# Two weight tiles of w_up split ahead of w_out's last rows, and one pair of attention heads scored a weight tile later, in a one-core hybrid decoder layer

## The chip, the cores and the metric

The kernel runs on one core of one Trainium2 chip. The metric is the time of one execution on the device in microseconds (us); the median of several runs is compared. TensorE is called PE here (PEld is its weight load), VectorE DVE, ScalarE ACT, GpSimd POOL; SP only issues transfers.

## What is computed

One decoder layer on 256 tokens of width 2048, all in float32. A norm, one wide projection, a state-space group and an attention group side by side, a second projection, a residual with a norm, and a squared-ReLU MLP:

```python
mix = hybrid_mixer(rmsnorm(h, norm_mix_pre), w_in, ..., w_out)   # concat(SSD, attention) @ w_out
h = h + rmsnorm(mix, norm_mix_post)
ff = squared_relu_mlp(rmsnorm(h, norm_mlp_pre), w_up, w_down)    # relu(u @ w_up)^2 @ w_down
h = h + rmsnorm(ff, norm_mlp_post)
...
s = where(mask, q @ k^T, -inf)          # attention: scores,
p = exp(s - max(s)); o = p @ v / sum(p) # probabilities, products with the values
```

w_in is 2048 x 12320, w_out 4096 x 2048, w_up 2048 x 8192, w_down 8192 x 2048.

## The kernel before

Every large product is made in split form. A float32 weight tile of 256 rows x 512 columns (two blocks of 128 rows) is fetched into a raw buffer, ACT rounds it to fp32r (hi, L144) and DVE takes the rest (lo, L145); the activations are kept as hi and lo too. A product is then hi*hi + hi*lo + lo*hi. There are four raw buffers (RAWS) and five pairs of hi and lo (BUFS). A raw buffer is free when DVE has made lo; a hi buffer is free when PE has done the matmuls that read it. SP issues the fetches in the order of the tiles.

Products come in two shapes. With features on the partitions (gemm_features, L474), one weight tile is sixteen matmuls, eight with hi (L468) and eight with lo (L471). With tokens on the partitions (row_tile, L317), one weight tile and one half of the tokens are six matmuls (L323 to L325).

**Where the attention is worked in.** gemm_features ends each of its eight weight tiles with pump(n): n pieces of waiting work are issued, and each piece that has more to do goes to the end of the queue. A pair of heads (attention, L842) is three pieces: scores (PE, L849 and L850, into two small PSUM buffers), followed by mask and maximum (DVE, L857), exponentials and their sums (ACT, L859), reciprocal and scaling (DVE, L861 and L863); then the transposes of the probabilities (PE, L871) and their copies (ACT, L875); then the products with the values (PE, L880 and L881) and their split. heads puts two such pairs into the queue. The small PSUM buffers are two, and they go round: the transposes of the first pair take those that the scores of the second pair filled. The tuple of pumps at L991, q2, says after which weight tiles of the queries' product a piece is issued; it repeats when it is shorter than eight. Other places have tuples of their own and are as they were.

**Where w_out passes over to w_up.** mix_to_up (L1055) ends w_out's last block of 512 columns and begins w_up. Its order is written out by hand and kept by every engine. It is made of small helpers: out(t, i) is the i-th of the last four weight tiles of w_out for half t of the tokens (tiles 2 and 3 lie in the buffer ua, which later holds the new activations); mix(t, n) adds the finished columns (DVE, L1080); mix_square takes their sum of squares (ACT, L1084); scale_of makes the mean (DVE, L1023) and its power -1/2 (POOL, L1024); weight multiplies by the norm's weights (L1087); add makes the new h (DVE, L1091); turn transposes it (PE, L1100); take splits it into the activations (ACT L146, DVE L147); rows(t, i) is a tile of w_up's first block. weigh(i) fetches w_up's tile i and splits it (ACT L144, DVE L145).

Of the kernel before, what the change touches and what calls it, by code (L numbers as in the profile page):

```python
# [35 lines left out]
COL_Q = COL_DT + 32  # L36
COL_K = COL_Q + NH * DH
COL_V = COL_K + NH * DH
NB = 512
# [38 lines left out]
def hymba_layer(ctx: ExitStack, tc: tile.TileContext, x, norm_mix_pre, w_in, conv_w, conv_b, dt_bias, a_log,  # L78
# [24 lines left out]
    def u(k):  # L103

        t, i = us[k]
        return t[:, i]
# [206 lines left out]
    def drain():  # L313
        while waiting:
            pump()
# [158 lines left out]
    def gemm_features(src, c0, begun=None, pumps=(1,)):  # L474


        acc = features()
        for k0 in range(0, NK, KB):
            hi, lo = weights(src, k0, c0) if k0 or begun is None else begun

            edges = k0 in (0, NK - KB)
            for fs in [(f,) for f in range(4)] if edges else [range(4)]:
                products(acc, hi, lo, k0, [(f, j) for f in fs for j in range(KB)])
            pump(pumps[k0 // KB % len(pumps)])
        return acc

    def added(dst, acc):

        with tc.high_priority(offset=AHEAD):
            for f, a in enumerate(acc):  # L490
                nc.scalar.activation(dst[:, f], a[:, 1], AF.Copy)
                nc.vector.tensor_tensor(dst[:, f], a[:, 0], dst[:, f], op=ALU.add)
# [139 lines left out]
    rbq = fp.tile([P, S], F32, name="rbq")  # L632
# [251 lines left out]
    def queries(c0, scale, pumps=(1,)):  # L884
        acc = gemm_features(w_in, c0, pumps=pumps)
        dst = mp.tile([P, 4, S], F32, name="cT", bufs=5)
        for b in range(2):
            d = dst[:, 2 * b:2 * b + 2]
            added(d, acc[2 * b:2 * b + 2])
            nc.vector.tensor_tensor(d, d, scale[:, None, :].to_broadcast([P, 2, S]), op=ALU.mult)  # L890
        return dst
# [76 lines left out]
    def heads(hb, qT, kT, v):  # L968
        for j in (0, 2):
            waiting.append(attention(ap, 4 * hb + j, qT[:, j:j + 2], kT[:, j:j + 2],  # L970
                                     v[:, :, j * DH:(j + 2) * DH].rearrange("p t (j d) -> p t j d", j=2)))
# [16 lines left out]
    qk.append(keys_by_tokens(1, (0, 2, 1, 4, 3, 7, 5), (6,), *eight))  # L988
    vs = two_values(0, *eight[::-1])
    heads(0, *qk[0], vs[0])  # L990
    q2 = queries(COL_Q + 2 * NB, rbq, (1, 1, 0))  # L991
    drain()
    heads(1, *qk[1], vs[1])
    qk.append((q2, queries(COL_K + 2 * NB, rbc, (1, 1, 0))))
# [19 lines left out]
    def sums_but_last(sums, t):  # L1014

        some = cp.tile([P, 1], F32, name="some", bufs=4)
        nc.vector.tensor_reduce(some, sums[:, t, 0:3], axis=mybir.AxisListType.X, op=ALU.add)
        nc.vector.tensor_scalar(some, some, D * EPS, None, op0=ALU.add)
        return some
# [35 lines left out]
    def mix_to_up(c0, ks, acc):  # L1055


        up = [bank() for _ in range(NT)]
        banks, turned = [], {}
        weighed = hp.tile([P, NT, NB], F32, name="e")  # L1060
        room_w = big.tile([P, SUMS, 2, S], F32R, name="ua").rearrange("p k b s -> p k (b s)")

        def tile_of(src, k, c0, at=None):
            raw = fetch(src, k * KB, c0)
            hi, lo = parts() if at is None else (room_w[:, at + KB * i:at + KB * (i + 1)] for i in range(2))
            split(hi, lo, raw)
            return hi, lo

        def out(t, i):
            row_tile(acc[1 + 2 * t], t, o[i], ks[i], part, False, i == len(ks) - 1)  # L1070

        def weigh(i):
            w[i] = tile_of(w_up, i % 8, i // 8 * NB)

        def rows(t, i):
            row_tile(up[t], t, w[i], i, act_u, i == 0, i == NK // KB - 1)

        def mix(t, n):
            m = mw_at(t, columns(n))
            nc.vector.tensor_tensor(m, acc[n - 2 + 2 * t], m, op=ALU.subtract if n % 2 else ALU.add)  # L1080

        def mix_square(t, n):
            junk = hp.tile([P, NB], F32, name="junk")
            nc.scalar.activation(junk, mw_at(t, columns(n)), AF.Square, accum_out=ssq[:, t, n:n + 1])  # L1084

        def weight(t, n):
            nc.vector.tensor_mul(mw_at(t, columns(n)) if n == 2 else weighed[:, t], mw_at(t, columns(n)), wpost[n])  # L1087

        def add(t, n):
            cs = columns(n)  # L1090
            nc.vector.scalar_tensor_tensor(of_h(t, cs), weighed[:, t] if n == 3 else mw_at(t, cs), rm[:, t:t + 1],  # L1091
                                           of_h(t, cs), op0=ALU.mult, op1=ALU.add)

        def turn(t, n):
            if len(banks) < 3:
                banks.append([bank() if banks else psmall() for _ in range(2)])
            p = turned[t, n] = banks[len(turned) % 3]
            for f in range(4):
                k = 4 * n + f
                nc.tensor.transpose(p[f % 2][:, f // 2 * P:(f // 2 + 1) * P], of_h(t, slice(k * P, (k + 1) * P)), ident)  # L1100

        def take(t, i):
            for k in (2 * i, 2 * i + 1):
                f = k % 4
                split(*(u(k)[:, b, t * P:(t + 1) * P] for b in range(2)),
                      turned[t, k // 4][f % 2][:, f // 2 * P:(f // 2 + 1) * P], w_mlp[:, k:k + 1])

        def square(t, n):
            junk = hp.tile([P, NB], F32, name="junk")
            nc.scalar.activation(junk, of_h(t, columns(n)), AF.Square, accum_out=ssh[:, t, n:n + 1])  # L1110

        o, w = {}, {}
        with tc.high_priority(offset=AHEAD), tc.manual_schedule():
            o[0] = tile_of(w_out, ks[0], c0)
            with tc.issue_after(product[0].ins), tc.issue_after(product[1].ins):
                out(0, 0)
            o[1] = tile_of(w_out, ks[1], c0)
            out(0, 1)
            o[2] = tile_of(w_out, ks[2], c0, 0)
            o[3] = tile_of(w_out, ks[3], c0, 4)  # L1120
            mix(0, 2)
            mix_square(0, 2)
            out(0, 2)
            mix(1, 2)
            mix_square(1, 2)
            first3[0] = sums_but_last(ssq, 0)
            first3[1] = sums_but_last(ssq, 1)
            out(0, 3)
            mix(0, 3)
            weight(0, 2)  # L1130
            weigh(0)
            out(1, 0)
            mix_square(0, 3)
            out(1, 1)
            scale_of(rm, ssq, first3[0], 0)
            weigh(1)
            add(0, 0)
            out(1, 2)
            add(0, 1)
            turn(0, 0)  # L1140
            weigh(2)
            square(0, 0)
            out(1, 3)
            new_u()
            take(0, 0)
            square(0, 1)
            mix(1, 3)
            turn(0, 1)
            take(0, 1)
            take(0, 2)  # L1150
            rows(0, 0)
            mix_square(1, 3)
            rows(0, 1)
            scale_of(rm, ssq, first3[1], 1)
            add(0, 2)
            take(0, 3)
            add(1, 0)
            weigh(3)
            square(0, 2)
            weight(1, 3)  # L1160
            rows(0, 2)
            add(1, 1)
            square(1, 0)
            turn(1, 0)
            turn(0, 2)
            take(1, 0)
            rows(0, 3)
            take(0, 4)
            take(1, 1)
            turn(1, 1)  # L1170
            rows(1, 0)
            square(1, 1)
            rows(1, 1)
            weight(1, 2)
            take(1, 2)
            add(1, 2)
            weigh(4)
            turn(1, 2)
            add(1, 3)
            take(0, 5)  # L1180
            take(1, 3)
            rows(1, 2)
            rows(0, 4)
            turn(1, 3)
            square(1, 2)
            weight(0, 3)
            add(0, 3)
            take(1, 4)
            rows(1, 3)
            weigh(5)  # L1190
            take(1, 5)
            weigh(6)
            turn(0, 3)
            rows(1, 4)
            rows(0, 5)
            take(1, 6)
            square(0, 3)
            weigh(7)
            take(0, 6)
            rows(1, 5)  # L1200
            take(0, 7)
            square(1, 3)
            rows(1, 6)
            scale_of(rmlp, ssh, sums_but_last(ssh, 0), 0)
            rows(0, 6)
            weigh(8)
            take(1, 7)
            rows(0, 7)
            rows(1, 7)
            scale_of(rmlp, ssh, sums_but_last(ssh, 1), 1)  # L1210
        for t in range(NT):
            waiting.append(first_hidden(t, up[t]))
        pump(NT)
        return w[8]
# [247 lines left out]
```

## Time and profile before

| | us |
|---|---|
| median of 3 runs | 1464.41 (1463.12 to 1464.65) |
| the profiled execution | 1462.01 |
| its span, first to last instruction | 1460.1 |
| PE busy | 1451.3 (99%) |
| DVE busy | 1254.7 (86%) |
| ACT busy | 888.7 (61%) |
| POOL busy | 143.1 (10%) |

The granted clock of PE is 0.999 of full speed over the whole span. A timeline row gives start, duration, engine, line, operation, what it writes and reads, and in brackets the idle time ahead of it with what ended it. Times count from the span's start. The attention of the first two pairs lies at about 447 to 473 us, the passage from w_out to w_up at about 757 to 800 us.

### The profile page before, as it was taken

The numbers are of one execution on the slowest core, as the hardware profiler recorded it, in microseconds if no ns is written. First come the engines' busy times: TensorE is split into PE (matmuls) and PEld (weight loads), VectorE is DVE, ScalarE is ACT, GpSimd is POOL, SyncE is SP. The second block draws the span as 40 slices with busy tenths as digits, with TensorE's granted clock in tenths as the row PEclk, the third lists the DMA queues.
The fourth block names the chain that finished last, engine by engine and source line by source line (L and its number), as shares of the span: only waits on it lengthen the run. The fifth ranks groups of instructions, "written<-read, shape, count | busy, mean of one in ns | idle before, by whom it ended". The sixth has DMA issues, their size and how long they took to land.

```text
span 1460.1 us, 20264 instructions
## 1 busy us (share of the span) xinstructions
PE 1451.3 (99%) x7129; PEld 1223.8 (84%) x7129; DVE 1254.7 (86%) x1864; ACT 888.7 (61%) x1214; POOL 143.1 (10%) x208
## 2 busy tenths in 40 slices
PE   9999999999999999999999999999999999999998
PEld 8888888888888888888887888888888888888886
DVE  6798797898887686689979999988889999999987
ACT  7475675465566555555557677655455776766553
POOL 0003100212010000000100011000111111001000
PEclk9999999999999999999999999999999999999999
DMA  8766666666886586688867798778888888797763
GB/s 273 209 204 180 180 184 192 175 180 184 226 241 206 134 245 199 192 265 253 253 190 241 202 315 240 217 214 230 246 236 271 263 244 250 204 308 238 251 212 116
DMA packets 168039, 323.53 MB, mean 222 GB/s; under 512 B 15185, under 2 KB 18113, under 8 KB 167937
## 3 DMA queue, kind: packets, MB, share of 16 engines
q1 hardware_dynamic: 144448, 272.37, 59.0%
q0 software_dynamic: 15616, 36.19, 12.3%
q10 hardware_dynamic: 7872, 13.68, 2.8%
q8 instruction: 56, 0.92, 0.2%
q14 instruction: 47, 0.38, 0.1%
HBM read 317.96 MB, written 40.41 MB: 245 GB/s over the span
## 4 chain that ended last, share of the span: by engine, by line
PE 99%; DVE 1%; ACT 0%; issue 0%; POOL 0%
PE acc L468 15%; PE acc L323 12%; PE acc L325 12%; PE acc L324 12%; PE acc L471 8%; PE acc L408 6%; PE acc L407 6%; PE acc L406 6%; PE ps L325 3%; PE ps L323 3%; PE ps L324 3%; PE ps L406 2%; PE ps L408 2%; PE ps L407 2%; PE ps L802 1%; PE acc L1375 1%
## 5 line engine op out<-in xcount | busy, mean ns | idle before, releaser
L144 ACT ACTIVATE hi<-raw 128x1024 fp32r<-128x1024 f32 (+1 forms) x408 | 427.1, 1051 | 293.0 <-PE acc L325 93.9
L145 DVE TENSOR_TENSOR lo<-raw,hi 128x1024 fp32r<-128x1024 f32 (+1 forms) x408 | 496.2, 1220 | 103.8 <-ACT hi L144 99.2
L468 PE MATMUL acc<-ua,hi 128*128 128x512 f32 x600 | 163.4, 401 | 0.0
L468 PEld LDWEIGHTS acc<-ua,hi 128*128 128x128 f32 x600 | 105.7, 189 | 16.7
L144 ACT ACTIVATE hi<-e 128x1024 fp32r<-128x1024 f32 x61 | 64.9, 1063 | 73.8 <-DVE e L247 67.4
L323 PE MATMUL acc<-hi,ua 128*128 128x512 f32 x248 | 98.5, 397 | 0.0
L471 PEld LDWEIGHTS acc<-ua,lo 128*128 128x128 f32 x600 | 88.2, 189 | 10.2
L325 PE MATMUL acc<-hi,ua 128*128 128x512 f32 x248 | 96.8, 390 | 0.0
L324 PE MATMUL acc<-lo,ua 128*128 128x512 f32 x248 | 96.7, 390 | 0.0
L471 PE MATMUL acc<-ua,lo 128*128 128x256 f32 x600 | 90.8, 281 | 0.0
L323 PE MATMUL acc<-hi,sh 128*128 128x512 f32 x224 | 88.4, 395 | 0.0
L325 PE MATMUL acc<-hi,sl 128*128 128x512 f32 x224 | 87.3, 390 | 0.0
L324 PE MATMUL acc<-lo,sh 128*128 128x512 f32 x224 | 87.2, 389 | 0.0
L145 DVE TENSOR_TENSOR lo<-e,hi 128x1024 fp32r<-128x1024 f32 x61 | 74.2, 1217 | 0.0
L468 PE MATMUL acc<-uc,hi 128*128 128x512 f32 x240 | 68.4, 397 | 0.0
L406 PE MATMUL acc<-hi,ah 128*128 128x512 f32 x166 | 64.7, 389 | 0.0
L407 PE MATMUL acc<-lo,ah 128*128 128x512 f32 x166 | 64.6, 389 | 0.0
L408 PE MATMUL acc<-hi,al 128*128 128x512 f32 x166 | 64.6, 389 | 0.0
L325 PE MATMUL acc<-hi,al 128*128 128x512 f32 x148 | 57.6, 389 | 0.0
L323 PE MATMUL acc<-hi,ah 128*128 128x512 f32 x148 | 57.6, 389 | 0.0
L324 PE MATMUL acc<-lo,ah 128*128 128x512 f32 x148 | 57.6, 389 | 0.0
L325 PEld LDWEIGHTS acc<-hi,ua 128*128 128x128 f32 x248 | 46.6, 188 | 10.0
(533 smaller groups left out, 3436.4 us busy)
## 6 DMA issues: line engine op xcount, KB each, us to landing
raw<-in_w_in_dram SPq DMA_DIRECT2D x181, 512.0 KB, 4.0
raw<-in_w_down_dram SPq DMA_DIRECT2D x73, 512.0 KB, 5.0
raw<-in_w_up_dram SPq DMA_DIRECT2D x65, 512.0 KB, 4.8
raw<-in_w_out_dram SPq DMA_DIRECT2D x39, 512.0 KB, 4.9
pair<-in_w_up_dram POOLq DMA_DIRECT2D x56, 256.0 KB, 5.3
raw<-pair SPq DMA_DIRECT2D x46, 256.0 KB, 4.5
pair<-in_w_down_dram POOLq DMA_DIRECT2D x46, 256.0 KB, 5.9
ha<-in_w_up_dram SPq DMA_DIRECT2D x20, 512.0 KB, 5.1
```

Of the source, the lines that this page charges most:

```text
L144: return (nc.scalar.activation(hi, src, AF.Copy), nc.vector.tensor_tensor(lo, src, hi.bitcast(F32), op=ALU.subtract))
L145: nc.vector.tensor_tensor(lo, src, hi.bitcast(F32), op=ALU.subtract))
L323: nc.tensor.matmul(dst, a_h[:, r, ts], hi[:, j], start=begin and j == 0, stop=False)
L324: nc.tensor.matmul(dst, a_h[:, r, ts], lo[:, j], start=False, stop=False)
L325: product[t] = nc.tensor.matmul(dst, a_l[:, r, ts], hi[:, j], start=False, stop=end and j == KB - 1)
L406: nc.tensor.matmul(dst, a_h, hi[:, j], start=own and first, stop=False)
L407: nc.tensor.matmul(dst, a_h, lo[:, j], start=False, stop=False)
L408: nc.tensor.matmul(dst, a_l, hi[:, j], start=False, stop=own and last)
L468: nc.tensor.matmul(acc[f], hi[:, j, f * P:(f + 1) * P], u(k0 + j), start=k0 + j == 0, stop=False, skip_group_check=True)
L471: nc.tensor.matmul(acc[f][:, 0], lo[:, j, f * P:(f + 1) * P], u(k0 + j)[:, 0], start=False, stop=k0 + j == NK - 1, skip_group_check=True)
L802: nc.tensor.matmul(p[:, c, r], bc[:, r, c * P:(c + 1) * P], xdt[:, c, r], start=True, stop=True)
L1375: nc.tensor.transpose(p[:, f * P:(f + 1) * P], r[:, f * P:(f + 1) * P], ident)
```

## The change

Two edits. In heads(0), which shares the queries' product q2, the pieces are issued after other weight tiles. Numbered from 0, before the first pair's pieces came after tiles 0, 3 and 6 and the second pair's after 1, 4 and 7; now the second pair's come after 2, 5 and 7, and the first pair's stay. In mix_to_up, weigh(0) and weigh(1) are issued ahead of out(0, 3), not behind weight(0, 2) and scale_of.

```diff
     heads(0, *qk[0], vs[0])
-    q2 = queries(COL_Q + 2 * NB, rbq, (1, 1, 0))
+    q2 = queries(COL_Q + 2 * NB, rbq, (1,0,1,1,0,1,1,1))
     drain()
...
             first3[0] = sums_but_last(ssq, 0)
             first3[1] = sums_but_last(ssq, 1)
+            weigh(0)
+            weigh(1)
             out(0, 3)
             mix(0, 3)
             weight(0, 2)
-            weigh(0)
             out(1, 0)
             mix_square(0, 3)
             out(1, 1)
             scale_of(rm, ssq, first3[0], 0)
-            weigh(1)
             add(0, 0)
```

DVE in mix_to_up, from the end of the partial sums (L1018) to the first two adds (L1091), before against now (mw is the mixed output, raw a weight tile as fetched, rmix the result of the power):

```order
 L1018 TENSOR_SCALAR some<-some 128x1
+L145 TENSOR_TENSOR lo<-raw,hi 128x1024 x2
 L1080 TENSOR_TENSOR mw_6121<-acc,mw_6121 128x512
 L1087 TENSOR_TENSOR mw_6120<-mw_6120,wpost 128x512
-L145 TENSOR_TENSOR lo<-raw,hi 128x1024
 L1023 TENSOR_SCALAR mean<-ssq,some 128x1
-L145 TENSOR_TENSOR lo<-raw,hi 128x1024
 L1091 SCALAR_TENSOR_TENSOR ha<-mw_6119,rmix,ha 128x512 x2
```

The two splits stood behind L1080, one on either side of the mean; now both stand ahead of L1080. ACT at the same place, before against now:

```order
 L1084 ACTIVATE junk,ssq<-mw_6120 128x512 x2
-L144 ACTIVATE hi<-raw 128x1024
+L144 ACTIVATE hi<-raw 128x1024 x2
 L1084 ACTIVATE junk,ssq<-mw_6121 128x512
-L144 ACTIVATE hi<-raw 128x1024 x2
+L144 ACTIVATE hi<-raw 128x1024
 L1110 ACTIVATE junk,ssh<-ha 128x512
```

Tile 0 was ahead of the sum of squares already; tile 1 joins it, and tile 2 stays behind.

PE in q2, from the scores of the first pair to the transposes of its probabilities, before:

```order
L849 MATMUL ps<-cT 128x128
L850 MATMUL ps<-cT 128x256
L468 MATMUL acc<-ua,hi 128x512 x8
L471 MATMUL acc<-ua,lo 128x256 x8
L849 MATMUL ps<-cT 128x128
L850 MATMUL ps<-cT 128x256
L849 MATMUL ps<-cT 128x128
L850 MATMUL ps<-cT 128x256
L468 MATMUL acc<-ua,hi 128x512 x8
L471 MATMUL acc<-ua,lo 128x256 x8
L468 MATMUL acc<-ua,hi 128x512 x8
L471 MATMUL acc<-ua,lo 128x256 x8
```

And now:

```order
L849 MATMUL ps<-cT 128x128
L850 MATMUL ps<-cT 128x256
L468 MATMUL acc<-ua,hi 128x512 x8
L471 MATMUL acc<-ua,lo 128x256 x8
L468 MATMUL acc<-ua,hi 128x512 x8
L471 MATMUL acc<-ua,lo 128x256 x8
L849 MATMUL ps<-cT 128x128
L850 MATMUL ps<-cT 128x256
L849 MATMUL ps<-cT 128x128
L850 MATMUL ps<-cT 128x256
L468 MATMUL acc<-ua,hi 128x512 x8
L471 MATMUL acc<-ua,lo 128x256 x8
```

Both pieces end where the transposes L871 of the first pair follow. The second pair's scores moved by one weight tile (an L468 row and an L471 row). DVE there, from the first pair's last maximum, now (before, all eight L857 of the two pairs stood together, and behind them one L145, both L861 and the four L863 of the first pair):

```order
L857 ISA mx 128x1
L145 TENSOR_TENSOR lo<-raw,hi 128x1024
L861 RECIPROCAL den<-den 128x2
L863 TENSOR_SCALAR sm<-sm,den 128x128
L145 TENSOR_TENSOR lo<-raw,hi 128x1024
L863 TENSOR_SCALAR sm<-sm,den 128x256
L861 RECIPROCAL den<-den 128x2
L857 ISA sm,mx<-ps,cst 128x128
L857 ISA mx 128x1
L863 TENSOR_SCALAR sm<-sm,den 128x128
L863 TENSOR_SCALAR sm<-sm,den 128x256
L857 ISA sm,mx<-ps,cst 128x256
```

A second weight tile's split now stands ahead of the second pair's maxima. What SP and POOL issue, and its order, is the same.

## The prediction

> **What bounds the kernel now.** I read the page first: share by engine, then the chain that ended last; then the waits of TensorE (PE) alone; then the timelines of the two places that the change touches.
>
> ```profile
> span 1460.1 us, 20264 instructions
> PE   1451.3 (99%) x7129; PEld 1223.8 (84%) x7129; DVE 1254.7 (86%) x1864; ACT 888.7 (61%) x1214; POOL 143.1 (10%) x208
> PE 99%; DVE 1%; ACT 0%; issue 0%; POOL 0%
> ```
>
> The first row after the span is busy time, the next the chain that ended last. PE fills 99% of both. An edit that only moves work on the other engines can win nothing but a wait of PE. These are all of them (engine, line, what it waited for: us in total, times, longest):
>
> ```profile
> PE ps L1320 <- ACT dg L1319: 2.0, 1, 2.0
> PE ps L519 <- DVE half L508: 1.1, 1, 1.1
> PE ps L1100 <- DVE ha L1091: 1.0, 1, 1.0
> PE acc L1100 <- DVE ha L1091: 0.2, 1, 0.2
> ```
>
> L1320 is the kernel's end and L519 its start; the change touches neither. The two waits at L1100 (turn, the transposes of the new h) lie in mix_to_up, where the weight tiles are moved. At the attention scores (L849, L850) PE has no wait in this list.
>
> **Part 1, the two weight tiles.** PE's timeline at both waits (start, duration, instruction, in brackets the idle time before it):
>
> ```profile
> 766.61 0.39 PE L325 MATMUL acc<-ua,al 128*128 128x512 f32 x1
> 767.95 0.66 PE L1100 MATMUL ps<-ident,ha 128*128 128x128 f32 x4 [0.95 <-DVE ha L1091]
> ...
> 769.59 0.39 PE L325 MATMUL acc<-ua,al 128*128 128x512 f32 x1
> 769.83 0.38 PE L1100 MATMUL acc<-ident,ha 128*128 128x128 f32 x2
> ...
> 774.45 0.39 PE L325 MATMUL acc<-hi,ua 128*128 128x512 f32 x1
> 775.07 0.66 PE L1100 MATMUL acc<-ident,ha 128*128 128x128 f32 x4 [0.23 <-DVE ha L1091]
> ```
>
> Matmuls overlap, so I count from start to start. Without a wait a turn starts 0.24 after the last matmul ahead of it (769.59 to 769.83). turn(0, 0) could have started at 766.61 + 0.24 = 766.85 and started at 767.95: **1.10 us lost**. The later turn(1, 0) lost 775.07 - 774.69 = 0.38. What the first one waited for:
>
> ```profile
> 759.24 0.15 DVE L1018 TENSOR_SCALAR some<-some 128x1 f32<-128x1 f32 x1
> 762.95 0.69 DVE L1080 TENSOR_TENSOR mw<-acc,mw 128x512 f32<-128x512 f32 x1 [3.56 <-PE acc L325]
> 763.56 0.68 DVE L1087 TENSOR_TENSOR mw<-mw,wpost 128x512 f32<-128x512 f32 x1
> 764.16 1.22 DVE L145 TENSOR_TENSOR lo<-raw,hi 128x1024 fp32r<-128x1024 f32 x1
> 765.29 0.21 DVE L1023 TENSOR_SCALAR mean<-ssq,some 128x1 f32<-128x1 f32 x1
> 765.45 1.23 DVE L145 TENSOR_TENSOR lo<-raw,hi 128x1024 fp32r<-128x1024 f32 x1
> 767.14 1.42 DVE L1091 SCALAR_TENSOR_TENSOR ha<-mw,rmix,ha 128x512 f32<-128x512 f32 x2 [0.47 <-POOL rmix L1024]
> ```
> ```profile
> 758.93 1.04 ACT L144 ACTIVATE hi<-raw 128x1024 fp32r<-128x1024 f32 x1
> 763.74 0.63 ACT L1084 ACTIVATE junk<-mw 128x512 f32<-128x512 f32 x1 [3.77 <-DVE mw L1080]
> 764.27 0.19 ACT L1084 ACTIVATION_READ_ACCUMULATOR junk<-mw 128x1 f32 x1
> 764.37 1.99 ACT L144 ACTIVATE hi<-raw 128x1024 fp32r<-128x1024 f32 x2
> ```
>
> The chain is mix (L1080), the sum of squares on ACT (L1084), mean (L1023), the power -1/2 on POOL (L1024), add (L1091), turn. L1084's sum is out at 764.27 + 0.19 = 764.46, but L1023 starts at 765.29: the split of tile 0 (L145, 764.16 + 1.22) is ahead of it in DVE's queue. Tile 1's split lies beside POOL:
>
> ```profile
> 765.59 1.51 POOL L1024 TENSOR_TENSOR rmix<-mean,half 128x1 f32<-128x1 f32 x1 [29.98 <-DVE mean L1023]
> 773.23 1.00 POOL L1024 TENSOR_TENSOR rmix<-mean,half 128x1 f32<-128x1 f32 x1 [6.12 <-DVE mean L1023]
> 792.17 0.54 POOL L1024 TENSOR_TENSOR rmlp<-mean,half 128x1 f32<-128x1 f32 x1 [17.94 <-DVE mean L1023]
> 792.74 0.29 DVE L627 TENSOR_SCALAR dg<-ident,rmlp 128x128 f32<-128x128 f32 x1 [0.65 <-POOL rmlp L1024]
> ```
>
> The same power takes 1.51 beside L145, 1.00 at 773.23, and 0.54 at 792.17, where DVE sits idle (0.65 before L627).
>
> With the change both splits go into the hole between L1018 (ends 759.39) and L1080 (762.95). ACT splits tile 0 at 758.93 as before, to 759.97, and tile 1 behind it, to 761.0; DVE follows from about 760.0, 1.22 each: 761.2 and 762.45. That is 0.5 us ahead of L1080. Is tile 1 there in time?
>
> ```profile
> 752.63 0.37 SPq L158 DMA_DIRECT2D raw<-in_w_up_dram  x1
> raw<-in_w_up_dram SPq DMA_DIRECT2D x7, 512.0 KB, 4.8
> ```
>
> It is asked for at 752.63 and lands 4.8 later (median), at 757.4. The order of the transfers stays; tiles 4 and 5 take over the two raw buffers and may be asked for 4 us earlier, which delays nobody ahead of them.
>
> New chain: L1023 at 764.48, POOL 0.30 later as before (765.29 to 765.59) at 764.78, 0.54 long, L1091 0.04 later at 765.36, turn 0.81 later (767.14 to 767.95) at 766.17. PE arrives at 766.85. The first wait goes whole, **-1.10**, with 0.68 of room; PE's own matmuls end last there then. If the power stayed at 1.51, turn could start at 767.14 and 0.29 would be left, a gain of 0.81. I take 0.54, since DVE is idle beside it as at 792.17; both ends stay for the range.
>
> The Trainium skill, SBUF — State Buffer, section "Who interferes with whom", says that a VectorE instruction with two inputs in SBUF shares a read port with a GpSimd instruction that reads SBUF, and that the later one blocks until the first has ended. The trace agrees: 765.45 + 1.23 + 0.54 = 767.22, against an end at 767.10. By that rule the sum is -1.10, without it -0.81.
>
> The second wait (0.38) hangs on a chain that begins with the end of out(1, 3), which moves with PE; the two tiles are no part of it. I take 0 for it, with -0.38 as the other end.
>
> **Part 2, the scores.** The second pair takes its scores one weight tile later (its probabilities are turned one tile later too); for the first pair nothing moves. PE does the same tiles and the same small matmuls in another order, so the count is unchanged, and a gain needs a wait, of which there is none. A loss needs a new one. The nearest place is the first pair's transposes (L871): they use the two small PSUM buffers that the second pair's scores have just filled, and had two weight tiles of room, now one.
>
> ```profile
> 451.00 0.39 PE L849 MATMUL ps<-cT 128*128 128x128 f32 x2
> ...
> 452.12 2.20 PE L468 MATMUL acc<-ua,hi 128*128 128x512 f32 x8
> ...
> 455.11 2.00 PE L468 MATMUL acc<-ua,hi 128*128 128x512 f32 x8
> ...
> 457.91 0.82 PE L871 MATMUL ps<-ident,sm 128*128 128x128 f32 x6
> ```
> ```profile
> 453.07 1.22 DVE L145 TENSOR_TENSOR lo<-raw,hi 128x1024 fp32r<-128x1024 f32 x1
> 454.21 0.22 DVE L861 RECIPROCAL den<-den 128x2 f32<-128x2 f32 x2
> 454.40 1.01 DVE L863 TENSOR_SCALAR sm<-sm,den 128x128 f32<-128x128 f32 x4
> ```
> ```profile
> 454.41 1.06 ACT L144 ACTIVATE hi<-raw 128x1024 fp32r<-128x1024 f32 x1 [1.14 <-issue]
> ```
>
> ACT's split at 454.41 follows the first half of tile 2 on PE (452.12 + 2.20 = 454.32), whose buffer it takes. Now tile 2 starts at 451.00 and its first half takes 2.00 (L468 takes 2.20 only behind scores), so the split runs from 453.1 to 454.15. Behind it on DVE stand L145 (to 455.4), the rest of the first pair's L861 and L863 (about 0.1 + 0.8) and the four L857 of the second pair. The first pair's four, first and last:
>
> ```profile
> 449.75 0.28 DVE L857 CUSTOM_DVE_ANT_0 sm<-ps,cst 128x128 f32<-128x128 f32 x1
> ...
> 450.51 0.42 DVE L857 CUSTOM_DVE_ANT_0 sm<-ps,cst 128x256 f32<-128x256 f32 x1
> ```
>
> From 449.75 to 450.51 + 0.42 = 450.93, four take 1.2, since they overlap; end to end, at 0.42 and less each, they would take 1.7 at most. The buffers come free at 455.4 + 0.9 + 1.2 = 457.5, at the worst 458.0. PE reaches the transposes at 457.91, as before, and the second buffer's 0.3 later. So **0**, with +0.1 as the upper end. Everything later (second transposes, products with v) has more than a tile of room.
>
> **Sum.** The profiled execution took 1462.01 us, span 1460.1 within it; 1462.01 - 1.10 = 1460.91. The median of the runs (1464.41) lies 2.40 above it, so I forecast 1464.41 - 1.10 = **1463.3 us**, 0.08% faster: less than the 0.2% that a measurement of this kernel can tell.
>
> **Rivals.**
> - The power stays long without its neighbour, or the splits slip: -0.81, 1463.6. Only the row at 765.59 speaks for it, and that row has L145 beside it. 9%.
> - The second wait goes too: -1.10 - 0.38 = -1.48, 1462.9. It would need DVE to reach mix(1, 3) sooner; but ACT holds that chain behind out(1, 3). 7%.
> - The gain is given back, or the change does not reach PE: 1464.4. It needs a later stage bound by a transfer; PE's list of waits has none. 7%.
> - The timed runs hold waits at these two places that the profiled one lacks. The second pair's scores start at 451.00, barely after the first pair's last L857 (450.93). If all of the 2.40 were of that kind, 1464.41 - 1.10 - 2.40 = 1460.9. Nothing shows it; the difference may as well be the launch. 9%.
> - **Slower:** the first pair's transposes wait. It decides where DVE's chain ends past 457.9, that is, 0.4 late. Let ACT's split get its buffer one weight tile (2.79, from the 455.11 tile to L871 at 457.91) later than I reckon: the chain ends at 457.5 + 2.8 = 460.3, PE loses 2.4, and with -1.10 the sum is +1.3, 1465.7. Some 4.4 late (2.9 + 1.1 + 0.4) would make it over 0.2%. Against it: the split at 454.41 starts 0.09 after tile 2's first half, so the buffer is that tile's. 6%.
>
> **Chances and range.** My forecast has 62%. Over 0.2% is 2.9 us: faster by so much only if most of the 2.40 goes too, 9%; slower only in the worst of the last case, 3%; within it 88%. The range holds the first four cases; the runs of before lie 1463.12 to 1464.65, 1.53 apart. From 1463.3 less that spread, 1461.8, to 1464.41 plus half of it, 1465.2.
>
> **What would show it.** PE's list of waits without the 1.0 at L1100, and the turn 0.24 after the matmul ahead of it; L145 twice between L1018 and L1080, and L1080 still straight after out(0, 3); POOL's power near 0.54; the 0.2 of turn(1, 0) still there; no wait at L871, and L871 7.0 us after tile 1's end as before (450.9 to 457.9). A wait at L871 or L849, L1080 late behind L145, or a power of 1.5 would prove a step wrong; a time beyond the range without such a row would mean that the profiled execution is not what the timed runs do.

## The result, and the profile after

The kernel before took 1464.43 us (median of 22 runs, 1462.21 to 1468.18), the changed one 1461.84 (22 runs, 1460.58 to 1464.08). The ratio is 0.9981, with a 95% interval of 0.9974 to 0.9987: 2.6 us or 0.19% faster, where 1.1 was forecast. The profiled execution of the changed kernel took 1460.96, 1.05 less than that of before. So the two profiled executions differ by what was forecast and the medians by 1.5 more: this 1.5 is what has to be explained.

PE's list of waits, changed kernel (engine, line, what it waited for: us in total, times, longest):

```profile
PE ps L1320 <- ACT dg L1319: 2.0, 1, 2.0
PE ps L519 <- DVE half L508: 1.1, 1, 1.1
PE acc L1100 <- DVE ha L1091: 0.2, 1, 0.2
```

The 1.0 at L1100 is gone, and nothing has come in its place. PE's timeline at the two turns, changed kernel:

```profile
766.88 0.39 PE L325 MATMUL acc<-ua,al 128*128 128x512 f32 x1
767.11 0.60 PE L1100 MATMUL ps<-ident,ha 128*128 128x128 f32 x4
...
773.57 0.39 PE L325 MATMUL acc<-hi,ua 128*128 128x512 f32 x1
774.18 0.66 PE L1100 MATMUL acc<-ident,ha 128*128 128x128 f32 x4 [0.22 <-DVE ha L1091]
```

The first turn starts 0.23 after the matmul ahead of it (1.34 before). The second turn still loses 0.38: 774.18 - 773.57 - 0.23. What DVE and POOL did ahead of the first turn, changed kernel:

```profile
760.28 2.36 DVE L145 TENSOR_TENSOR lo<-raw,hi 128x1024 fp32r<-128x1024 f32 x2 [0.60 <-ACT hi L144]
763.23 0.69 DVE L1080 TENSOR_TENSOR mw<-acc,mw 128x512 f32<-128x512 f32 x1 [0.59 <-PE acc L325]
...
764.77 0.21 DVE L1023 TENSOR_SCALAR mean<-ssq,some 128x1 f32<-128x1 f32 x1 [0.25 <-ACT junk L1084]
765.67 1.42 DVE L1091 SCALAR_TENSOR_TENSOR ha<-mw,rmix,ha 128x512 f32<-128x512 f32 x2 [0.69 <-POOL rmix L1024]
```
```profile
765.07 0.57 POOL L1024 TENSOR_TENSOR rmix<-mean,half 128x1 f32<-128x1 f32 x1 [29.30 <-DVE mean L1023]
```

Both splits end at 762.64, 0.59 ahead of L1080, and the power takes 0.57 (1.51 before). At the attention nothing waits in this execution either. PE's rows of the first pair's scores, the second pair's scores and the first pair's transposes, changed kernel:

```profile
447.17 0.38 PE L849 MATMUL ps<-cT 128*128 128x128 f32 x2
...
454.07 0.39 PE L849 MATMUL ps<-cT 128*128 128x128 f32 x2
...
458.18 0.82 PE L871 MATMUL ps<-ident,sm 128*128 128x128 f32 x6
```

From the first to the second pair's scores it is 6.90 now. In the kernel before the second pair's stood at 451.00, and the first pair's at:

```profile
446.89 0.38 PE L849 MATMUL ps<-cT 128*128 128x128 f32 x2
```

That is 4.11 apart, one weight tile less.

### The profile page after: what moved, and what is told of

Read it like the earlier page. It is cut to its first block, busy times and chain, and to the rows that moved or that the text cites. A ratio compares the mean times of both kernels' runs of the same rounds, so it can differ in the third digit from the quotient of the medians.

```text
span 1459.1 us, 20265 instructions
## 1 busy us (share of the span) xinstructions
PE 1451.2 (99%) x7129; PEld 1224.0 (84%) x7129; DVE 1255.9 (86%) x1864; ACT 890.2 (61%) x1214; POOL 142.1 (10%) x208
## 4 chain that ended last, share of the span: by engine, by line
PE 99%; DVE 0%; ACT 0%; issue 0%
PE acc L468 15%; PE acc L323 12%; PE acc L325 12%; PE acc L324 12%; PE acc L471 8%; PE acc L406 6%; PE acc L407 6%; PE acc L408 6%; PE ps L323 3%; PE ps L325 3%; PE ps L324 3%; PE ps L406 2%; PE ps L407 2%; PE ps L408 2%; PE ps L802 1%; PE acc L1375 1%
## 5 line engine op out<-in xcount | busy, mean ns | idle before, releaser
L145 DVE TENSOR_TENSOR lo<-raw,hi 128x1024 fp32r<-128x1024 f32 (+1 forms) x408 | 496.7, 1221 | 101.8 <-ACT hi L144 97.3
L468 PE MATMUL acc<-ua,hi 128*128 128x512 f32 x600 | 163.6, 401 | 0.0
L468 PEld LDWEIGHTS acc<-ua,hi 128*128 128x128 f32 x600 | 105.7, 189 | 16.8
L471 PEld LDWEIGHTS acc<-ua,lo 128*128 128x128 f32 x600 | 88.2, 189 | 10.2
L471 PE MATMUL acc<-ua,lo 128*128 128x256 f32 x600 | 90.8, 281 | 0.0
L145 DVE TENSOR_TENSOR lo<-e,hi 128x1024 fp32r<-128x1024 f32 x61 | 74.3, 1218 | 0.0
L468 PE MATMUL acc<-uc,hi 128*128 128x512 f32 x240 | 68.5, 397 | 0.0
```

What stands on the lines that cost most here:

```text
L145: nc.vector.tensor_tensor(lo, src, hi.bitcast(F32), op=ALU.subtract))
L468: nc.tensor.matmul(acc[f], hi[:, j, f * P:(f + 1) * P], u(k0 + j), start=k0 + j == 0, stop=False, skip_group_check=True)
L471: nc.tensor.matmul(acc[f][:, 0], lo[:, j, f * P:(f + 1) * P], u(k0 + j)[:, 0], start=False, stop=k0 + j == NK - 1, skip_group_check=True)
```

## Experiments

Each ratio is to the kernel before, run beside it on the same chip; its interval is 95%.

**One half of the change at a time.** e1 has the new order of mix_to_up and the old table of q2, e2 the new table and the old order. The diffs are against the changed kernel; each takes one half of the change back:

```diff
 e1:
-    q2 = queries(COL_Q + 2 * NB, rbq, (1,0,1,1,0,1,1,1))
+    q2 = queries(COL_Q + 2 * NB, rbq, (1, 1, 0))
```
```diff
 e2:
-            weigh(0)
-            weigh(1)
             out(0, 3)
             mix(0, 3)
             weight(0, 2)
+            weigh(0)
...
             scale_of(rm, ssq, first3[0], 0)
+            weigh(1)
```

> Only the two weight tiles are moved; the scores stand as before. Theory T (the timed runs hold a wait at the second pair's scores that the profiled execution of before happened not to have): this part gives its 1.1 us and no more, ratio about 0.9992; the profile has no first wait at L1100, power 0.54 to 0.6, and it may show PE waiting at L849, up to 1.5 us, since the scores still stand where a late DVE is felt. Rival U (the tiles give it all, because the wait at L1100 is longer in the timed runs): ratio about 0.9981. Rival V (the rest of the gain over 1.1 is scatter between sets of runs): 0.9992, and no wait at L849 in any profile.

> Only the scores are moved; the weight tiles stand as before. T: ratio about 0.9990, that is 1.5 us, though a single profile may show nothing of it; wait of 1.0 at L1100 as before, none at L849 or L871. U: 1.000. V: 1.000.

| | median, us | runs | ratio to before |
|---|---|---|---|
| e1, tiles only | 1462.63 (1460.84 to 1467.94) | 12 | 0.9991 [0.9982, 1.0] |
| e2, scores only | 1463.01 (1461.55 to 1464.01) | 11 | 0.9988 [0.9979, 0.9996] |
| e4, both (the changed kernel) | 1461.50 (1460.49 to 1463.99) | 11 | 0.998 [0.9972, 0.9989] |
| before, beside them | 1464.27 (1462.20 to 1466.86) | 35 | 1 |

The scores alone are worth 1.3 to 1.8 us (from the medians and from the ratio), where the forecast had 0; the tiles alone 1.3 to 1.6, though e1's interval reaches to 1.0, so that its gain rests on its profile as well; the two add up to that of both. Rivals U and V are out: both ask for 1.000 in e2, whose interval ends at 0.9996. Nor is it the granted clock of PE: of the 35 runs of the kernel before, the 21 at 0.999 have a median of 1463.99, and all eleven of e4, at 0.999 too, one of 1461.50. e1's list of waits of PE shows a wait that the list of before doesn't have:

```profile
PE ps L849 <- DVE mx L857: 0.6, 1, 0.6
```

L849 is the second pair's scores in their old place. e2's list has the 1.0 at L1100 and no wait at L849.

**The two kernels once more,** unchanged (e3 is the kernel before, e4 the changed one), for a second profile of each.

> The kernel of before, unchanged, for the scatter and a second profile of it. All theories: ratio 1.000 within its interval. T: the profile's wait at L849 lies anywhere between 0 and 2 us, and goes with the time at which the first pair's last L857 ends against the tile that PE has just finished: no wait where DVE is as early as in the first profile (0.07 ahead), a wait where it is later. U and V: no wait there.

> The changed kernel, unchanged, beside the two halves on the same chip. T and U: about 0.9981; V: about 0.9992. T: no wait at L849 nor at L871, however late DVE is with the first pair's L857 (1.7 late in its first profile). If T holds, the two halves add up to this one.

e3 took 1464.46 (11 runs, ratio 1.0001, 0.9993 to 1.001), e4 as in the table. PE's waits in the second profile of the same kernel as before:

```profile
PE ps L849 <- DVE mx L857: 2.4, 1, 2.4
...
PE ps L1100 <- DVE ha L1091: 0.9, 1, 0.9
```

The largest wait of this execution, 2.4 at L849, a little above the 0 to 2 that I expected, is not in the first profile at all. The rows of e3 that lead to it, ACT, then DVE, then PE:

```profile
444.70 1.06 ACT L144 ACTIVATE hi<-raw 128x1024 fp32r<-128x1024 f32 x1 [4.14 <-DMA raw<-in_w_in_dram]
```
```profile
448.13 3.68 DVE L145 TENSOR_TENSOR lo<-raw,hi 128x1024 fp32r<-128x1024 f32 x3
452.76 1.23 DVE L145 TENSOR_TENSOR lo<-raw,hi 128x1024 fp32r<-128x1024 f32 x1 [0.95 <-ACT hi L144]
453.90 0.28 DVE L857 CUSTOM_DVE_ANT_0 sm<-ps,cst 128x128 f32<-128x128 f32 x1
...
454.11 0.42 DVE L857 CUSTOM_DVE_ANT_0 sm<-ps,cst 128x256 f32<-128x256 f32 x1
```
```profile
447.93 0.38 PE L849 MATMUL ps<-cT 128*128 128x128 f32 x2
...
454.60 0.49 PE L849 MATMUL ps<-cT 128*128 128x128 f32 x2 [2.40 <-DVE mx L857]
```

Read from above: ACT sits idle 4.14 for a weight tile; the splits of the weights behind it fill DVE's queue; the first pair's masks and maxima (L857) stand behind those splits; the first of the two small PSUM buffers is free when the first head's two L857 have ended (454.11 + 0.42 = 454.53); the second pair's scores start 0.07 later. Without a wait they would have come at 447.93 + 4.11 = 452.04, so 2.56 are lost. In the profile of before the same rows read:

```profile
439.72 1.06 ACT L144 ACTIVATE hi<-raw 128x1024 fp32r<-128x1024 f32 x1 [1.82 <-DVE lo L145]
```
```profile
448.61 1.23 DVE L145 TENSOR_TENSOR lo<-raw,hi 128x1024 fp32r<-128x1024 f32 x1 [0.20 <-ACT hi L144]
...
449.96 0.42 DVE L857 CUSTOM_DVE_ANT_0 sm<-ps,cst 128x256 f32<-128x256 f32 x1
```

There the same tile was rounded 4.98 earlier, with no wait for a transfer, while the first scores on PE were only 1.04 earlier. The buffer was free at 450.38 and the scores started at 451.00: 0.56 of room, if 0.06 lie between release and start (0.06 in e1, 0.07 in e3). Up to the first pair's L857 DVE, ACT and PE run the same instructions in the same order in the old and the new order, so every profile without an extra transfer can be asked the same: how long after the first pair's scores (L849) is the buffer free, and how long would the old order, with its 4.11 less 0.06, have waited? That wait is an estimate for all but the first kernel, e1 and e3, which have the old order. The last column is the median time from issue to landing of the weight tiles (512 KB each) that SP asks for between 433 and 442 us, the last ones whose splits stand ahead of L857.

| profile | buffer free after, us | old order would wait | weight tiles land after, us |
|---|---|---|---|
| before | 3.49 | 0 | 4.5 |
| e1 | 4.76 | 0.71 (it did, 0.71) | 6.4 |
| the changed kernel | 4.87 | 0.82 | 4.9 |
| e2 | 5.19 | 1.14 | 6.9 |
| e5 (below) | 5.51 | 1.46 | 7.1 |
| e4 | 5.70 | 1.65 | 5.3 |
| e10 (below) | 5.81 | 1.76 | 6.6 |
| e3 | 6.60 | 2.55 (it did, 2.56) | 6.8 |
| e8 (below) | 6.69 | 2.64 | 6.2 |

The mean of the estimated waits is 1.4. The first profile, on which the prediction rests, is the most favourable of the nine, and its weight tiles land soonest; the order of the others is not that of their landing times, so these tiles are not the whole of it. In e4's profile the six transposes, which stand one weight tile behind the scores, take 1.10 in place of 0.82:

```profile
459.01 1.10 PE L871 MATMUL ps<-ident,sm 128*128 128x128 f32 x6
```

So the new order can lose some tenths there, without a wait that the list shows.

**Which half of the 1.1 us is the queue, which the power?** e5 puts the second tile's split back behind scale_of:

```diff
             weigh(0)
-            weigh(1)
             out(0, 3)
...
             scale_of(rm, ssq, first3[0], 0)
+            weigh(1)
```

> The changed kernel with the second weight tile's split back behind scale_of; the first tile's stays ahead of the column block, and the scores stay two tiles on. On VectorE the row is then L145, L1080, L1087, L1023, L145, L1091. It asks which half of the 1.1 us the queue took and which the power on GpSimd. The theory of the prediction (queue and port): the mean L1023 is not held up, the power L1024 starts ahead of the second L145 and takes about 0.57; but L1091 stands behind L145, which starts when ScalarE's split of the tile ends (about 765.7) and takes 1.22: L1091 at about 766.85, turn at 767.66 against 767.11 without a wait, so a wait of 0.5 at L1100 and a time 0.5 above that of the changed kernel (about 1462.3). Rival 1, the first tile alone was the cause: no wait at L1100 beside the later 0.2, and the time of the changed kernel. Rival 2, the power stays long beside any L145: power 1.2 to 1.5 and a wait of 0.8 to 1.1.

DVE, POOL and PE in e5:

```profile
764.89 0.21 DVE L1023 TENSOR_SCALAR mean<-ssq,some 128x1 f32<-128x1 f32 x1 [0.25 <-ACT junk L1084]
765.84 1.23 DVE L145 TENSOR_TENSOR lo<-raw,hi 128x1024 fp32r<-128x1024 f32 x1 [0.74 <-ACT hi L144]
766.98 1.41 DVE L1091 SCALAR_TENSOR_TENSOR ha<-mw,rmix,ha 128x512 f32<-128x512 f32 x2
```
```profile
765.19 0.57 POOL L1024 TENSOR_TENSOR rmix<-mean,half 128x1 f32<-128x1 f32 x1 [28.20 <-DVE mean L1023]
```
```profile
767.00 0.39 PE L325 MATMUL acc<-ua,al 128*128 128x512 f32 x1
767.78 0.66 PE L1100 MATMUL ps<-ident,ha 128*128 128x128 f32 x4 [0.39 <-DVE ha L1091]
```

The power is over (765.76) before L145 starts, and takes 0.57; but L1091 stands behind L145 in DVE's queue, and the turn loses 767.78 - 767.00 - 0.23 = 0.55. So of the 1.1 us, half goes with the first tile alone, and the other half is the add behind the second split. For the kernel before, an estimate from these rows: L1091 starts 1.14 after its L145 in e5, which from 765.45 is 766.59, and it started at 767.14, so that the long power added 0.55 and the queue alone the rest. Rival 1 is out. Rival 2 is not tested by e5, in which no L145 runs beside the power. The time was 1462.14 (12 runs, ratio 0.9984, 0.9975 to 0.9994), between e2's and the changed kernel's, too near both for the runs to tell.

**Is it the weights' lateness?** e6 (the kernel before) and e7 (the changed one) issue one more transfer, 512 KB that nothing reads, behind a weight tile of the values:

```diff
-        return raw
+        return extra() or raw
...
+    def extra():
+        room["spare"] = room.get("spare", 0) - 1
+        with tc.issue_after(loaded[0].ins): room["spare"] or nc.sync.dma_start(dram.tile([KB * P, NB], F32, name="spare_d"), w_in[0:KB * P, 0:NB])
...
-    vs = two_values(0, *eight[::-1])
+    room["spare"] = 12; vs = two_values(0, *eight[::-1])
```

> The kernel before with one more transfer on SyncE's queue: 512 KB from the weights to a spare place in DRAM, which nothing reads, behind the second last weight tile of the values that is asked for before 430 us. It delays the weight tiles behind it. Theory (the old place of the scores has no room, so what comes late from DRAM is paid at L849): the last weight tiles of the values land 1.5 to 3.5 us later, ScalarE's and VectorE's splits follow, the first pair's last L857 ends that much later than 450.93, and TensorE waits at L849 for 1.5 to 3.5 us; the time is 1 to 3 us above that of before (1465.4 to 1467.4). Rival, transfers have nothing to do with it (VectorE's chain is late for another reason, or has room): the wait at L849 is within the 0 to 2.6 that was seen without the transfer and the time within 0.5 of before.

> The changed kernel with the same transfer of 512 KB at the same place of SyncE's queue. Theory: the second pair's scores have one weight tile more of room (0.6 to 1.5 us were left in the profiles of the new order), so of a delay of 1.5 to 3.5 us only what goes beyond that is paid: a wait of 0 to 2 us at L849, and a time 0 to 1.5 us above that of the changed kernel (1461.6 to 1463.2); the distance to the kernel before with the transfer grows from 2.6 to 3 to 5 us. Rival, the delay is paid elsewhere (the product of the values waits for its weights, or everything is late alike): both kernels lose the same, and the distance stays at 2.6.

e6 took 1465.30 (12 runs, ratio 1.0012, 1.0001 to 1.0024), 0.1 short of the expected range, e7 1463.07 (12 runs, 0.9991, 0.9983 to 0.9999); before, beside them, 1463.96 (35 runs). So 512 KB cost both kernels about the same, 1.3 and (against e4's 1461.50, from another chip) 1.6 us, and their distance stayed at 2.2: the growth to 3 to 5 that I expected did not come, and the rival's "both kernels lose the same" did. One of PE's waits in e7 says where the changed kernel paid:

```profile
PE ps L871 <- DVE mx L857: 1.4, 1, 1.4
```

The new order has paid too, at another place, as its PE rows show:

```profile
447.34 0.38 PE L849 MATMUL ps<-cT 128*128 128x128 f32 x2
...
454.33 0.49 PE L849 MATMUL ps<-cT 128*128 128x128 f32 x2
...
460.14 1.10 PE L871 MATMUL ps<-ident,sm 128*128 128x128 f32 x6 [1.43 <-DVE mx L857]
```

The second pair's scores come 6.99 after the first pair's, 0.09 late. The transposes stand one weight tile behind them and need the buffer back from the second pair's L857, which stand behind the same late splits; PE sits idle there for 1.43. e6's own profile has 0.3 at L849; that profile is of the shortest of its 12 executions (1463.15, against a median of 1465.30), so that the cost of e6 rests on its times, not on its rows, and where it was paid is not shown.

**The same with more room for the transposes.** e9 is e7 with the first pair's transposes one weight tile further on, e11 is e7 once more beside it:

```diff
-    q2 = queries(COL_Q + 2 * NB, rbq, (1,0,1,1,0,1,1,1))
+    q2 = queries(COL_Q + 2 * NB, rbq, (1,0,1,0,1,1,1,1))
```

> The changed kernel with the extra transfer of 512 KB, and the first pair's transposes (L871) one weight tile further on: the table of the second query block is (1,0,1,0,1,1,1,1) in place of (1,0,1,1,0,1,1,1). With the transfer and the changed table TensorE waited 1.4 us at L871 for the second pair's L857, which ended at 460.64, where the transposes would have stood at 458.6. Theory (the lateness of the weights is one delay that the attention steps meet at whichever place has least room): a weight tile more moves L871 to about 461.4, the wait at L871 goes, what is left at L849 is 0 to 0.3, and the time comes down by 1 to 1.5 from the 1463.1 that the changed kernel with the transfer took, to 1461.6 to 1462.1. Rival (the transfer is paid elsewhere too, by weights that TensorE itself waits for): the wait at L871 goes, but the time stays within 0.5 of 1463.1.

> The changed kernel with the extra transfer once more, beside the two others on the same chip: 1463.1 as before (1462.5 to 1463.7), with a wait at L871 or L849 of 0 to 1.5 us in its profile, since how late the weights come differs between executions.

e11 took 1463.53 (11 runs, ratio 0.9991, 0.9982 to 1.0), e9 1461.87 (11 runs, 0.9979, 0.997 to 0.9988); before, beside them, 1464.82 (24 runs). e11's waits at the attention, and then e9's:

```profile
PE ps L871 <- DVE mx L857: 0.9, 1, 0.9
PE ps L849 <- DVE mx L857: 0.7, 1, 0.7
```
```profile
PE ps L849 <- DVE mx L857: 0.4, 1, 0.4
```

With the same transfer, moving the first pair's small transposes by one weight tile gives 1.66 us of the median back (the two intervals still share 0.0006, but nine of e9's eleven times lie below ten of e11's eleven), and the wait at L871 is gone. So a good part of what the late weights cost is paid where an attention step has no room. Not all of it: e9 is still 0.9 above e10, the same kernel without the transfer (below), though the intervals of the two overlap, and its profile shows 0.4 at L849. In the four profiles with the transfer (e6, e7, e9, e11) the buffer at L849 is free 4.51, 6.93, 7.35 and 7.67 after the first scores, 6.6 on average against 5.4 in the nine of the table.

**Without the extra transfer.** e10 is the changed kernel with that table alone; e8 has the table and one more edit of the other kind, square(0, 1) moved on ACT from ahead of the second half's mix_square(1, 3) to behind it.

> The changed kernel with the table (1,0,1,0,1,1,1,1) and no extra transfer: the first pair's transposes one weight tile further on, nothing else moved. If runs of the changed kernel still lose time at L871 now and then (its profiles showed 0 and 0.2 there, and its times reach 3 us above the lowest), the median falls by 0.1 to 0.5, to 1461.1 to 1461.5, and the longest times come down. If L871 has room in nearly all of them, the median stays at 1461.5 to 1461.8.

> The changed kernel with two more shifts of the same two kinds: the first pair's transposes (L871) one weight tile further on, and square(0, 1) on ScalarE moved from ahead of mix_square(1, 3) to behind it, so that the sum of squares of the second rows' block, and with it L1023, L1024, L1091 and turn(1, 0), come up to 0.47 earlier. If room at these places is what counts: the 0.2 at the second L1100 goes (0.38 from start to start), and the 0.2 that was lost at L871 in one profile of the changed kernel; together 0.4 to 0.6 less, 1461.0 to 1461.4. The scheduler also moves some instructions of VectorE around the start of the second half of the up product (L364 to L492), which may give or cost some tenths. If the places have room already: the time of the changed kernel, 1461.6.

```diff
 e8, beside e10's table:
             take(0, 0)
-            square(0, 1)
             mix(1, 3)
...
             mix_square(1, 3)
+            square(0, 1)
```

e10 took 1460.96 (8 runs beside e9's, 1460.59 to 1462.21; ratio 0.9974, 0.9964 to 0.9985), a little below the 1461.1 to 1461.5 expected, e8 1461.27 (12 runs beside e5's, 1460.61 to 1463.10; 0.998, 0.9971 to 0.9988). All waits of PE in e8:

```profile
PE ps L1320 <- ACT dg L1319: 2.0, 1, 2.0
PE ps L519 <- DVE half L508: 1.1, 1, 1.1
```

The second wait at L1100 is gone as well, and the span is 1458.7, the shortest of the profiled executions. e10 has the lowest median of all kernels, and its longest run is below the longest of any other; but the intervals of e10, e8 and the changed kernel overlap, so that only "faster than before" is shown for them, not an order among the three.

## Why the prediction was wrong

**What held.** The term of Part 1, -1.10. The first wait went whole (1.34 to 0.23 from the matmul to the turn), the splits ended 0.59 ahead of L1080 (0.5 forecast), the power took 0.57 (0.54 forecast), the second wait stayed at 0.38. e1 measures the tiles alone at 1.3 (ratio) to 1.6 (medians). The first wait, unlike the scores', hardly changes between executions: 1.34 from the matmul to the turn in e2 and 1.33 in e6, which have the old order of mix_to_up. The rule quoted there from the Trainium skill (SBUF — State Buffer, "Who interferes with whom": a GpSimd instruction that reads SBUF and a VectorE one with two inputs in SBUF exclude each other) agrees with these rows: the power takes 1.51 or 1.52 in the four profiles in which L145 runs beside it (before, e2, e3, e6), and 0.57 in the nine others.

**What failed** is Part 2's step "a gain needs a wait, of which there is none", so the 0 of the scores in the sum. e2 measured the scores alone at 1.3 to 1.8 us. The wait at L849 is there in the second profile of the same kernel (2.56) and in e1 (0.71), 1.4 us on average by the table's estimate, and not in the one execution that I read. Two steps led past it. I took the list of waits of one execution for a property of the kernel. And I measured the room of the new order at L871, but not that of the old order at L849, where the scores start 0.6 after their buffer is free, behind a DVE queue that depends on transfers. That the measured 1461.84 still lies in the range is luck: its lower end, 1461.8, is the spread of three runs below the forecast and stands for no mechanism.

**The rival** "the timed runs hold waits at these two places that the profiled one lacks" had it, at 9%, and named the place, without a row to show it. It priced it at all of the 2.40 us by which the median lay above the profiled execution. The changed kernel's median lies 0.88 above its own profiled execution (1461.84 against 1460.96), with no wait at these places; taken as other scatter (PE's busy time alone runs from 1451.0 to 1452.4 over the thirteen profiles), it leaves 2.40 - 0.88 = 1.5 for the scores' wait. That is the subtraction of the result over again and no second measurement; e2 and the table are. It also spoke of the last L857 (450.93) as the release; the buffer is free with the second (450.38). e7's expectation counts the room of the new order from the last one too: from the second it is 1.1 to 2.0 in the three profiles, not 0.6 to 1.5.

**The slower rival** (transposes wait) did not decide the result, but its mechanism is real: with weights later by an extra 512 KB, L871 waited 1.4 and 0.9 us in two profiles, and without it e4's transposes took 0.28 longer. The prediction gave that place 0.4 of room and asked for a buffer 2.8 late to fill it; transfers alone can do that.

**What stays open** is why the weights come at such different times. The pair sums that POOL issues (L271, L272) each wait for the transfer before them, so lateness can add up there. One of these waits in the kernel before, then in e3:

```profile
421.91 0.56 POOL L271 DMA_DIRECT2D pair<-in_w_in_dram  x1 [6.35 <-DMA raw<-pair]
```
```profile
426.49 0.56 POOL L271 DMA_DIRECT2D pair<-in_w_in_dram  x1 [7.85 <-DMA raw<-pair]
```

It is 1.5 longer in e3 and this sum starts 4.58 later, while PE is only 1.04 later at the first scores (447.93 against 446.89). The other profiles follow this only in part: e5's starts at 422.60, ahead of e1's at 423.30, and its buffer is free later. That is a reading of profiles; no run took these transfers away.

## What to carry to other kernels

A list of waits belongs to one execution: where the median lies above the profiled execution, look for the places whose room is smaller than the scatter of the transfers ahead of them, and take a second profile before pricing an edit there at nothing. Room is read from the release of the buffer to the start of its next user, on both sides of the change, and each step moved takes the lateness on to the next place with the least room.

## What the runs showed of the hardware

Weight tiles came at times that differ by microseconds from one execution to the next: those asked for between 433 and 442 us landed after 4.5 to 7.1 us (medians), and the same buffer was free 3.49 to 6.69 us after the same matmul, in nine profiles that run the same instructions up to there. One more transfer of 512 KB among the weights, which no engine reads, made the kernel before 1.3 us longer, and 0.9 the one with most room (e9 against e10, whose intervals overlap). A power on POOL over 128x1 took 0.57 us in nine profiles and 1.51 or 1.52 in the four in which a two-input DVE instruction of 1.2 us ran beside it.
